# Reading x with features in the partitions, and weaving the first three projections over the tiles of u

## The chip, the cores and the metric

The kernel runs on one core of one Trainium2 chip. The metric is the device time of one execution in microseconds (us). The engines have the names of the profile: PE is TensorE (matmul), PEld its weight loads, DVE is VectorE, ACT is ScalarE, POOL is GpSimd and SP is SyncE, which issues most of the DMAs.

## The reference

One layer of a streaming encoder on 512 frames of 1024 features, float32: a normalised input u, one combined projection of it, three branches (gated linear attention "GLA", forgetting attention "FoX", attention into 256 memory tokens), a gated merge, and a squared-ReLU MLP. What matters here is the head of it.

```python
def rmsnorm(x, g):
    r = lax.rsqrt(jnp.mean(xf * xf, axis=-1, keepdims=True) + EPS)
    return (xf * r) * g

u = rmsnorm(h, g_mix[l])                 # h = x, 512 x 1024
proj = u @ w_in[l]
(gq, gk, gv, gg, ga, fq, fk, fv, ff, mq, gates) = split_cols(proj, PROJ_SIZES)
log_a = jax.nn.log_sigmoid(ga @ w_alpha_up[l] + b_alpha[l]) / GLA_TAU
log_f = jax.nn.log_sigmoid(ff + b_forget[l])      # decay of FoX
...
mkv = rmsnorm(mem, g_mem[l]) @ w_mem_kv[l]        # memory keys and values
mk, mv = jnp.split(mkv, 2, axis=-1)
```

## The kernel before

All matrix products are done in three passes of a short float format: each operand is split into a high part (a cast on ACT) and a low part (operand minus high part, on DVE), and PE adds high x high, high x low and low x high in PSUM. Weights come in chunks of 128 x 1024 numbers (512 KB), in the order of `chunk_list()`: a DMA on SP's queue writes a tile `raw` (three buffers, or two of the tag `lead`), ACT writes `hi` or `whi`, DVE writes `lo` or `wlo` (three buffers each).

The head of the kernel, with which this change deals, has these parts.

- Memory keys, `mem_keys` (L380): chunks 0 to 3, 96 matmuls of 256 columns.
- Memory values, `mem_values` (L394): chunks 4 to 7. For each chunk PE does two units of four matmuls with the high part and two units of two matmuls with the low part, 48 matmuls in all. A unit ends at a `yield`, so other code can decide how many units run between two of its own steps (`run(islice(mv, 2))`).
- u. x is read frame by frame (`xn`: 128 frames in the partitions, four tiles). ACT squares a tile and sums it along the row (L330), DVE and POOL make the factor (mean plus epsilon, to the power of -0.5; L333 and L334), and DVE scales the tile by a factor that is one number for each partition (L340). PE then turns it (L408): 32 transposes of 128 x 128, four for each of the eight tiles `k` of 128 features. ACT and DVE write `uhi` and `ulo` from PSUM (L411, L412), with the gain `g_mix` that is then one number for each partition.
- `g_proj` (L504, L505): the columns of the decays (chunk G: `ga` and `ff`), 16 matmuls. It comes when all of u is there. Then `fox_pair(0)` by `gT` and `mm3` (L157 to L159): the first 128 query columns and the first 128 key columns of FoX (fq, fk), 24 matmuls each. Then `decay_logs` (L520) and FoX's values (fv, four chunks).

PE runs its instructions in the order in which the code is written. On the other engines a scheduler sets the order, which `issue_after` and helpers like `behind` bind in places. `hold[0]` names an instruction on ACT after which later casts of weights are put. `next_sum` lets one sum of weights in DRAM (POOL's queue) go with each cast of a chunk from the 12th call on; they serve the MLP.

Of the kernel before, what the change touches and what calls it, by code (L numbers as in the profile page):

```python
# [32 lines left out]
def chunk_list():  # L33

    L = []
    for c in (0, 512):
        L += [("N", "w_mem_kv", 2 * j, c) for j in range(4)]
    L += [("G",)]
    L += [("T", "w_in", OFF["fq"]), ("T", "w_in", OFF["fk"])]
# [24 lines left out]
def hybrid_block(ctx, tc, chunks, wst, memT, xN, gffn, gfin, wup, cst, out):  # L64
# [57 lines left out]
    def next_sum(after):  # L122
# [3 lines left out]
        if n <= 11:  # L126
            return
        for to, src, add_ in islice(sums[len(late_on)], 1 + (len(late_on) == 1)):
            with tc.issue_after(merged[0]) if late_on else ExitStack():
                if add_:  # L130
                    d = nc.gpsimd.dma_start(to, src, accum_op=ALU.add, max_dma_last_dim=8192)
                else:
                    d = nc.gpsimd.dma_start(to, src)
            tc.add_manual_dep(d.ins, after.name, mybir.DependencyInfo(mybir.DependencyClass.Sync, mybir.DependencyReason.DATA),
                              reason="pace")

# [16 lines left out]
    def get_w(key):  # L153
        return split_w(load_w(key))
# [98 lines left out]
    with pool("front") as fp:  # L253
# [4 lines left out]
        xn = fp.tile([P, NT, D], F32, name="xn")  # L258
        ssx = small(fp, NT, "ssx")
# [61 lines left out]
        load, act, vec = next(lead(chunks[4], after=(load, act, vec)))  # L321

        def x_load(t):
            with behind(load):
                return nc.sync.dma_start(xn[:, t, :], xN[t * P:(t + 1) * P, :]).ins

        def x_square(t):
            sq = fp.tile([P, D], F32, tag="xsq", name=nm("xsq"), bufs=2)
            with behind(act):
                a = nc.scalar.activation(sq, xn[:, t, :], AF.Square, accum_out=ssx[:, t:t + 1]).ins  # L330
            ms, r = (fp.tile([P, 1], F32, tag=g, name=nm(g), bufs=2) for g in ("ms", "rr"))
            with behind(vec):
                m = nc.vector.tensor_scalar(ms, ssx[:, t:t + 1], 1.0 / D, EPS, op0=ALU.mult, op1=ALU.add).ins  # L333
            nc.gpsimd.tensor_tensor(r, ms, mhalf[:, :1], op=ALU.pow)  # L334
            return a, m, r

        def x_scale(t, r, cols=(0, D)):
            for sl in (slice(a, b) for a, b in zip(cols, cols[1:])):
                with behind(vec):
                    v = nc.vector.tensor_scalar(xn[:, t, sl], xn[:, t, sl], r, None, op0=ALU.mult).ins  # L340
            return v

        for t in range(2):
            load = x_load(t)
            act, vec, r = x_square(t)
            if t == 0:
                vec = x_scale(t, r)
        load, act, vec = next(lead(chunks[5], after=(load, act, vec)))
        load = x_load(2)
        act, vec, r2 = x_square(2)  # L350
        vec = x_scale(1, r)
        vec = x_scale(2, r2)
        load = x_load(3)
        act, vec, r = x_square(3)
        x_scale(3, r, (0, 2 * P, D))
        x_act = act
        with behind(load):
            nc.sync.dma_start(ident, cst[:, :P])
        get_plain = get_w

        def get_first(key):
            return pre[key] if key in pre else get_plain(key)

        get_w = get_first
# [18 lines left out]
        def mem_values():  # L383
            pss = [at_() for _ in range(2)]
            for j in range(4):
                with behind(u_mid if j == 3 else None):
                    w = [x.rearrange("p (k c) -> p k c", k=2) for x in get_w(("N", "w_mem_kv", 2 * j, 512))]
                for low in range(2):
                    for t, ps in enumerate(pss):
# [6 lines left out]
                        if j == 3 and low:  # L396
                            with tc.issue_after(u_end):
                                nc.vector.tensor_copy(gqT[t], ps)
                        yield

        def k_copies(after, hs):
            with tc.issue_after(after):
                for h in hs:
                    nc.scalar.copy(mk_raw(h), kps[h])

        def turn(pt, k, ts):
            for t in ts:
                nc.tensor.transpose(pt[:, t * P:(t + 1) * P], xn[:, t, k * P:(k + 1) * P], ident)  # L408

        def u_split(pt, k):  # L410
            a = nc.scalar.mul(uhi[:, k, :], pt, gmix[:, k:k + 1]).ins  # L411
            return a, nc.vector.scalar_tensor_tensor(ulo[:, k, :], pt, gmix[:, k:k + 1], f(uhi[:, k, :]), op0=ALU.mult,  # L412
                                                  op1=ALU.subtract).ins
# [3 lines left out]
        k_copies(x_act, (0, 1))  # L417
        mv = mem_values()
        macc, rm, dg = gv[:, 2, :M], gv[:, 1, :2], gv[:, 3, :M]
        msq = [fp.tile([P, 4, M], F32, name=f"msq{h}") for h in range(2)]  # L420
        u_act = None
        run(islice(mv, 8))
        pts, u_mid = [at_() for _ in range(2)], None
        for ts in (range(NT - 1), (NT - 1,)):
            for k in range(2):
                turn(pts[k], k, ts)
        for k in range(KT):
            if k > 1:
                pts.append(at_())
                turn(pts[k], k, range(NT))  # L430
            u_act, u_end = u_split(pts[k], k)
            u_mid = u_act if k == 3 else u_mid
            u_late = u_act if k <= 5 else u_late
            if k in (1, 3, 5):
                run(islice(mv, 2))
            if k in (5, 7):
                h = k // 7
                with tc.issue_after(u_act):
                    nc.scalar.activation(msq[h], memr[:, 4 * h:4 * h + 4, :], AF.Square)
        k_copies(u_act, (2, 3))  # L440
        run(mv)
        hold[0] = u_late
        get_w = get_plain
# [1344 lines left out]
```

## Time and profile before

| | us |
|---|---|
| median of 3 runs | 815.97 |
| lowest and highest | 814.61, 816.88 |
| the profiled execution, its own time | 815.5 |
| its span | 813.7 |

The span runs from the first to the last instruction of the trace. The profiled execution's own time is 1.8 us longer than its span. All "us" in lines of the profile are counted from the start of the span. In a line of the timeline the first two numbers are the start and the length. Matmul lines overlap, since their ends are modelled; where the time that PE spends is wanted, take the difference of two starts. In the profile's names `T<-a,b` means that T is written from a and b.

### The profile page before, as it was taken

The numbers are of one execution on the slowest core, as the hardware profiler recorded it, in microseconds if no ns is written. First come the engines' busy times: TensorE is split into PE (matmuls) and PEld (weight loads), VectorE is DVE, ScalarE is ACT, GpSimd is POOL, SyncE is SP. The second block draws the span as 40 slices with busy tenths as digits, with TensorE's granted clock in tenths as the row PEclk, the third lists the DMA queues.
The fourth block names the chain that finished last, engine by engine and source line by source line (L and its number), as shares of the span: only waits on it lengthen the run. The fifth ranks groups of instructions, "written<-read, shape, count | busy, mean of one in ns | idle before, by whom it ended". The sixth has DMA issues, their size and how long they took to land.

```text
span 813.7 us, 12505 instructions
## 1 busy us (share of the span) xinstructions
PE 803.3 (99%) x4813; PEld 706.9 (87%) x4813; DVE 591.3 (73%) x913; ACT 442.0 (54%) x699; POOL 109.0 (13%) x135
## 2 busy tenths in 40 slices
PE   8999999999999999999999999999999999999996
PEld 7788888888888888999999889987998899889984
DVE  5856878546455587877567468788788778887896
ACT  7745655543344334444454346874676367637764
POOL 0000110011101112134144110011001100100011
PEclk9999999999999999999999999999999999999998
DMA  9534666688888877767768733998758966896643
GB/s 354 168 118 139 190 177 200 184 236 200 252 236 273 232 227 184 170 165 196 199 148 225 247 98 130 279 233 232 239 163 200 222 210 167 194 281 193 160 82 125
DMA packets 39484, 161.29 MB, mean 198 GB/s; under 512 B 4736, under 2 KB 5184, under 8 KB 37056
## 3 DMA queue, kind: packets, MB, share of 16 engines
q0 software_dynamic: 9776, 58.20, 34.3%
q1 hardware_dynamic: 27856, 97.55, 34.1%
q10 hardware_dynamic: 1792, 4.75, 1.7%
q8 instruction: 37, 0.61, 0.3%
q14 instruction: 23, 0.19, 0.1%
HBM read 158.35 MB, written 35.68 MB: 238 GB/s over the span
## 4 chain that ended last, share of the span: by engine, by line
PE 92%; DVE 3%; ACT 2%; DMA 2%; issue 1%; POOL 0%; POOLq 0%; DVEq 0%; ACTq 0%
PE mm L1233 18%; PE mm L157 17%; PE mm L158 17%; PE mm L159 17%; PE a L157 5%; PE a L158 4%; PE a L159 4%; PE mm L380 1%; PE a L394 1%; DMA b<-in_wst_dram 1%; ACT hi L1357 1%; DVE lo L1291 1%; PE a L624 1%; DVE h L1285 1%; PE a L662 1%
## 5 line engine op out<-in xcount | busy, mean ns | idle before, releaser
L148 DVE TENSOR_TENSOR wlo<-raw,whi 128x1024 fp32r<-128x1024 f32 x65 | 84.1, 1296 | 58.4 <-ACT whi L147 58.2
L157 PE MATMUL mm<-uhi,whi 128*128 128x512 f32 (+1 forms) x352 | 125.8, 357 | 0.0
L159 PE MATMUL mm<-uhi,wlo 128*128 128x512 f32 (+1 forms) x352 | 123.7, 351 | 0.0
L158 PE MATMUL mm<-ulo,whi 128*128 128x512 f32 (+1 forms) x352 | 123.6, 351 | 0.0
L147 ACT CAST whi<-raw 128x1024 fp32r<-128x1024 f32 x65 | 68.4, 1052 | 89.2 <-PE mm L158 54.4
L1289 ACT CAST hi<-raw 128x1024 fp32r<-128x1024 f32 x56 | 58.8, 1050 | 45.1 <-PE mm L1233 30.2
L1291 DVE TENSOR_TENSOR lo<-raw,hi 128x1024 fp32r<-128x1024 f32 x56 | 68.5, 1223 | 14.6 <-ACT hi L1289 14.6
L157 PEld LDWEIGHTS mm<-uhi,whi 128*128 128x128 f32 x352 | 66.7, 189 | 9.9 <-issue 1.5
L159 PEld LDWEIGHTS mm<-uhi,wlo 128*128 128x128 f32 x352 | 66.6, 189 | 9.1
L158 PEld LDWEIGHTS mm<-ulo,whi 128*128 128x128 f32 x352 | 66.7, 189 | 8.1
L1233 PE MATMUL mm<-u2l,hi 128*128 128x256 f32 x240 | 66.1, 283 | 0.0
L1233 PE MATMUL mm<-u2h,hi 128*128 128x256 f32 x240 | 66.1, 283 | 0.0
L1233 PE MATMUL mm<-u2h,lo 128*128 128x256 f32 x240 | 61.1, 283 | 0.0
L1643 POOL DMA_DIRECT2D b<-in_wst_dram x30 | 25.6, 854 | 264.2 <-DVE lo L1291 153.3
L1289 ACT CAST hi<-b 128x1024 fp32r<-128x1024 f32 x36 | 37.8, 1049 | 38.1 <-PE mm L159 24.0
L158 PE MATMUL mm<-lo,ch 128*128 128x512 f32 x136 | 53.0, 390 | 0.7 <-DVE lo L1291 0.7
L157 PE MATMUL mm<-hi,ch 128*128 128x512 f32 x136 | 52.9, 389 | 0.0
L159 PE MATMUL mm<-hi,cl 128*128 128x512 f32 x136 | 52.9, 389 | 0.0
L1233 PE MATMUL mm<-u2sh,hi 128*128 128x256 f32 x192 | 52.6, 283 | 0.0
L1233 PE MATMUL mm<-u2sl,hi 128*128 128x256 f32 x192 | 52.5, 283 | 0.0
L1291 DVE TENSOR_TENSOR lo<-b,hi 128x1024 fp32r<-128x1024 f32 x36 | 43.9, 1221 | 10.4 <-ACT hi L1289 10.2
L1233 PE MATMUL mm<-u2sh,lo 128*128 128x256 f32 x192 | 47.5, 283 | 0.0
(423 smaller groups left out, 2105.7 us busy)
## 6 DMA issues: line engine op xcount, KB each, us to landing
raw<-in_wst_dram SPq DMA_DIRECT2D x113, 512.0 KB
raw<-T SPq DMA_DIRECT2D x32, 512.0 KB
b<-in_wst_dram POOLq DMA_DIRECT2D x32, 512.0 KB, 5.6
T<-in_wst_dram POOLq DMA_DIRECT2D x12, 1024.0 KB, 9.0
b<-in_wst_dram SPq DMA_DIRECT2D x16, 512.0 KB
wb<-in_wst_dram POOLq DMA_DIRECT2D x15, 512.0 KB, 5.4
T<-in_wst_dram POOLq DMA_DIRECT2D x12, 512.0 KB, 5.7
wb<-in_wst_dram SPq DMA_DIRECT2D x8, 512.0 KB
```

The lines of the kernel that those rows point to most:

```text
L147: cast = nc.scalar.copy(hi, raw)
L148: low_now[0] = nc.vector.tensor_tensor(lo, raw, f(hi), op=ALU.subtract).ins
L157: nc.tensor.matmul(ps, lh, rh, start=start, stop=False, skip_group_check=on)
L158: nc.tensor.matmul(ps, lh, rl, start=False, stop=False, skip_group_check=on)
L159: nc.tensor.matmul(ps, ll, rh, start=False, stop=stop, skip_group_check=on)
L380: nc.tensor.matmul(kps[h], w[:, h * P:(h + 1) * P], x[:, k, :], start=k == p == 0, stop=k == KT - 1 and p == 2)
L394: nc.tensor.matmul(ps, x[:, k, sl], w[low][:, kk, :], start=k == low == 0 and x is mxh, stop=k == KT - 1 and low == 1)
L624: nc.tensor.matmul(ps[e], q[a, sl], k[a, :w], start=p == 0, stop=p == 2)
L1233: nc.tensor.matmul(ps[:, a, :], x[:, a, k, :], y[:, s, k, :], start=start, stop=stop, skip_group_check=go is not None)
L1289: nc.scalar.copy(hi, raw)
L1291: nc.vector.tensor_tensor(lo, raw, f(hi), op=ALU.subtract)
L1643: nc.gpsimd.dma_start(to[i], wst[index["B", q, i, x]], accum_op=ALU.add)
```

## The change

x is given twice, as before (`xN`, for the residual) and with features in the partitions (`xT`). The head of the kernel reads `xT` into `xt` (eight tiles of 128 features x 512 frames, two to a DMA), so u needs no transposes. In exchange, the sum of squares runs over partitions:

- ACT squares `xt` (four DMAs' worth; the last in two halves) and DVE adds the eight tiles into one (`x_sum`, L346 and L350 of the new kernel).
- PE adds that tile's partitions, by four matmuls with a column of ones (L429), DVE adds epsilon (L430), and POOL makes all four factors of a partition in one instruction (`rx`, L431). PE then makes of them a row that stands in all partitions (`rb`, four transposes of a broadcast column, L436).
- DVE multiplies each tile of `xt` by `rb` (`x_scale`, L440), ACT writes `uhi` (L443), DVE writes `ulo` (L446).

The projections of fq, fk and G, which were done one after the other, are woven: as soon as tile k of u is there, PE does the matmuls of fq and fk with it (high weights only, L602), and from k = 2 on also the two matmuls of G with tile k-2 (L514, L515). The low weights of fq and fk come last, eight matmuls each (L611). The weights fq, fk and G are loaded and cast earlier. DVE, ACT and SP run in this part in the order in which the code is written (`in_order`, which existed before and is moved up). The copies of the memory values go from DVE to ACT. `hold[0]` is now the copy of the decay columns, and `next_sum` starts at the eighth call, because four chunks no longer go through `split_w`.

```diff
-    L += [("G",)]
     L += [("T", "w_in", OFF["fq"]), ("T", "w_in", OFF["fk"])]
+    L += [("G",)]
...
-        if n <= 11:
+        if n <= 7:
...
-        def x_square(t):
-            sq = fp.tile([P, D], F32, tag="xsq", name=nm("xsq"), bufs=2)
-            with behind(act):
-                a = nc.scalar.activation(sq, xn[:, t, :], AF.Square, accum_out=ssx[:, t:t + 1]).ins
...
+        order = in_order()
+        order.__enter__()
+        next(lead(chunks[4], after=(load, act, vec)))
+        def x_load(j):
+            nc.sync.dma_start(xt[:, 2 * j:2 * j + 2, :].rearrange("p k t -> p (k t)"), xT[j])
+        def x_square(j):
+            sq = fp.tile([P, 2, S], F32, tag="xsq", name=nm("xsq"), bufs=3)
+            for k in range(2) if j == 3 else [slice(0, 2)]:
+                nc.scalar.activation(sq[:, k], xt[:, 2 * j:2 * j + 2, :][:, k], AF.Square)
+            if j == 1:
+                nc.vector.tensor_tensor(sq, sq, sqs[0], op=ALU.add)
...
+        vraws = [fp.tile([P, 1024], F32, tag="lead", name=nm("raw"), bufs=2) for _ in range(2)]
+        nc.sync.dma_start(vraws[0], wst[6])
+        nc.sync.dma_start(ident, cst[:, :P])
+        nc.sync.dma_start(vraws[1], wst[7])
+        fraws = [load_w(("T", "w_in", OFF[n])) for n in ("fq", "fk")]
+        g_raw = load_w(("G",))
...
-        def turn(pt, k, ts):
-            for t in ts:
-                nc.tensor.transpose(pt[:, t * P:(t + 1) * P], xn[:, t, k * P:(k + 1) * P], ident)
...
+        lead_w(chunks[6], vraws[0])()
+        run(islice(mv, 9))
+        lead_w(chunks[7], vraws[1])()
+        ps = at_()
+        for t in range(NT):
+            nc.tensor.matmul(ps[:, t:t + 1], ssum[:, t * P:(t + 1) * P], ones[:, 0:1], start=True, stop=True)
+        nc.vector.tensor_scalar(ms, ps[:, :NT], 1.0 / D, EPS, op0=ALU.mult, op1=ALU.add)
+        nc.gpsimd.tensor_tensor(rx, ms, mhalf[:, :NT], op=ALU.pow)
+        k_copies(range(4))
+        run(islice(mv, 3))
+        rb = at_()
+        for t in range(NT):
+            nc.tensor.transpose(rb[:, t * P:(t + 1) * P], rx[:, t:t + 1].to_broadcast([P, P]), ident)
+        lows = [lead_w(chunks[8 + n], fraws[n]) for n in range(2)]
...
         for k in range(KT):
+            x_scale(k)
+            u_high(k)
+            if k:
+                u_low(k - 1)
+            if k == 1:
+                gw = wp.tile([P, 1024], F32R, tag="hi", name=nm("whi"))
+                nc.scalar.copy(gw, g_raw)
+            if k == 3:
+                nc.vector.tensor_tensor(gw3[:, :, 64:], gr3[:, :, 64:], f(gw3[:, :, 64:]), op=ALU.subtract)
+        u_low(KT - 1)
+        run(islice(mv, 2))
...
+        def first_pair():
+            for k in range(KT):
+                for u in (uhi, ulo):
+                    if k == 0:
+                        run(islice(mv, 1))
+                    for w, ps in zip(ws, pss):
+                        nc.tensor.matmul(ps, w[0][:, k, :], u[:, k, :], start=k == 0 and u is uhi, stop=False)
+                if k > 1:
+                    g_tile(k - 2)
...
+            for w, ps, evac in zip(ws, pss, evacs):
+                for k in range(KT):
+                    nc.tensor.matmul(ps, w[1][:, k, :], uhi[:, k, :], start=False, stop=k == KT - 1)
+                evac(ps)
```

How the instructions stand, at three places. First DVE between the low part of chunk 4 and the first low part of u, before. `ms` and `rr` are the mean square and the factor of one tile of 128 frames; `lo_236` is the low part of chunk 5, `wlo_406` that of chunk 6.

```order
L276 TENSOR_TENSOR lo_215<-raw_213,hi_214 128x1024
L333 TENSOR_SCALAR ms_222<-ssx_138 128x1
L340 TENSOR_SCALAR xn<-xn,rr_223 128x1024
L333 TENSOR_SCALAR ms_230<-ssx_138 128x1
L276 TENSOR_TENSOR lo_236<-raw_234,hi_235 128x1024
L333 TENSOR_SCALAR ms_243<-ssx_138 128x1
L340 TENSOR_SCALAR xn<-xn,rr_231 128x1024
L340 TENSOR_SCALAR xn<-xn,rr_244 128x1024
L333 TENSOR_SCALAR ms_252<-ssx_138 128x1
L340 TENSOR_SCALAR xn<-xn,rr_253 128x256
L340 TENSOR_SCALAR xn<-xn,rr_253 128x768
L148 TENSOR_TENSOR wlo_406<-raw_403,whi_405 128x1024
```

The same engine from the low part of chunk 5 (`lo_228`) on, now: `xsq_222` is the sum of squares, `lo_362` and `lo_396` are the low parts of chunks 6 and 7, `a_399` is the PSUM tile of the column sums, `a_418` is `rb`.

```order
L288 TENSOR_TENSOR lo_228<-raw_226,hi_227 128x1024
L350 TENSOR_TENSOR xsq_248<-xsq_248 128x512
L350 TENSOR_TENSOR xsq_222<-xsq_222,xsq_248 128x512
L350 TENSOR_TENSOR xsq_222<-xsq_222,xsq_251 128x512 x2
L416 TENSOR_TENSOR lo_362<-raw_234,hi_361 128x1024
L416 TENSOR_TENSOR lo_396<-raw_235,hi_395 128x1024
L430 TENSOR_SCALAR ms_359<-a_399 128x4
L440 TENSOR_TENSOR xt<-xt,a_418 128x512 x2
L446 SCALAR_TENSOR_TENSOR ulo<-xt,cols_s,uhi 128x512
L440 TENSOR_TENSOR xt<-xt,a_418 128x512
L446 SCALAR_TENSOR_TENSOR ulo<-xt,cols_s,uhi 128x512
```

The low parts of both chunks 6 and 7 now stand ahead of the one `ms`, and from the scaling on DVE alternates between two instructions for each tile of u.

Second PE, where the values' chunk 5 ends and u begins, before (`a_363` and `a_364` are the two tiles of memory values, `a_389` and `a_390` take the first two tiles of u).

```order
L394 MATMUL a_363<-lo_236,mxh 128x512 x2
L394 MATMUL a_364<-lo_236,mxh 128x512 x2
L408 MATMUL a_389<-cst_s,xn 128x128 x3
L408 MATMUL a_390<-cst_s,xn 128x128 x3
L408 MATMUL a_389<-cst_s,xn 128x128
L408 MATMUL a_390<-cst_s,xn 128x128
L394 MATMUL a_363<-whi_405,mxh 128x512
```

And now, from the column sums to the row of factors, in the middle of chunk 6 (`hi_361`, `lo_362`).

```order
L429 MATMUL a_399<-ones,xsq_222 128x1 x4
L403 MATMUL a_366<-hi_361,mxh 128x512
L403 MATMUL a_366<-hi_361,mxl 128x512
L403 MATMUL a_366<-hi_361,mxh 128x512
L403 MATMUL a_366<-hi_361,mxl 128x512
L403 MATMUL a_365<-lo_362,mxh 128x512 x2
L403 MATMUL a_366<-lo_362,mxh 128x512 x2
L436 MATMUL a_418<-cst_s,rx_360 128x128 x4
```

Eight matmuls of the memory values now stand between the column sums and the row, and the rest of the values (chunk 7, 12 matmuls) after it; the 32 transposes are gone.

Third ACT, around the first tiles of u, before (`whi_405` and `whi_451` are chunks 6 and 7, `a_389` and so on are tiles of u in PSUM).

```order
L147 CAST whi_405<-raw_403 128x1024
L411 ACTIVATE uhi<-a_389,cols_s 128x512
L411 ACTIVATE uhi<-a_390,cols_s 128x512
L411 ACTIVATE uhi<-a_417,cols_s 128x512
L411 ACTIVATE uhi<-a_424,cols_s 128x512
L147 CAST whi_451<-raw_449 128x1024
```

And now (`hi_423` and `hi_426` are fq and fk, `whi_434` is G, `gqT` takes the memory values).

```order
L415 CAST hi_423<-raw_239 128x1024
L415 CAST hi_426<-raw_241 128x1024
L443 ACTIVATE uhi<-xt,cols_s 128x512 x2
L456 CAST whi_434<-raw_243 128x1024
L406 COPY gqT_114<-a_365 128x512
L443 ACTIVATE uhi<-xt,cols_s 128x512
L406 COPY gqT_115<-a_366 128x512
L443 ACTIVATE uhi<-xt,cols_s 128x512 x5
```

The cast of G and the two copies of the values now stand between the second and the fourth tile of `uhi`. On all engines the order behind FoX's first values is the one of before.

More of the change, by code (lines that the diff above doesn't have):

```diff
@@ L337, in x_scale @@
[L337 to L348, printed above, removed]
```

181 lines of the change are left out of this document (80 added, 101 removed).

## Prediction

> **What bounds the kernel now.** I read the page first (busy shares, the chain that ended last), then the busy time by stage, then the timeline of the first 50 us engine by engine.
>
> ```profile
> PE 803.3 (99%) x4813; PEld 706.9 (87%) x4813; DVE 591.3 (73%) x913; ACT 442.0 (54%) x699; POOL 109.0 (13%) x135
> ...
> PE 92%; DVE 3%; ACT 2%; DMA 2%; issue 1%; POOL 0%; POOLq 0%; DVEq 0%; ACTq 0%
> ```
>
> The first line is the busy time of each engine, the second the share of each in the chain that ended last. The stages, each line with the stage's bounds, its length, the busy time and count of PE, PEld, DVE, ACT and POOL, the granted clock of PE, the busy share of the DMA engines and GB/s:
>
> ```profile
> 17.40:33.00 15.60, 15.59 (x83) 12.15 (x82) 10.87 (x16) 11.53 (x19) 1.49 (x2) 1.00 0.62 221
> 33.00:47.50 14.50, 14.50 (x66) 12.00 (x66) 10.77 (x14) 6.72 (x12) 0.35 (x2) 1.00 0.55 183
> 47.50:550.00 502.50, 502.50 (x2968) 438.94 (x2967) 342.46 (x590) 250.81 (x434) 81.07 (x92) 1.00 0.70 197
> 550.00:555.00 5.00, 4.26 (x19) 3.21 (x18) 5.00 (x7) 2.07 (x3) 0.85 (x1) 1.00 0.62 207
> 555.00:805.00 250.00, 249.94 (x1575) 227.03 (x1575) 209.03 (x261) 155.07 (x209) 22.41 (x27) 1.00 0.72 192
> 805.00:813.70 8.70, 1.30 (x6) 0.75 (x4) 2.53 (x5) 2.29 (x6) 1.10 (x2) 0.76 0.31 121
> ```
>
> PE is the bound: between 17.4 and 805 us PE waits for 0.8 us in all, 0.74 of them near 550. So whatever PE work leaves the head moves the end by as much, and each us that PE waits in the new head costs a us. Everything behind FoX's first values stands in the same order on every engine, so I let the rest shift as it is, the short wait at 550 included: DVE and transfers that run there start from work that shifts along.
>
> **What leaves PE.**
>
> ```profile
> 17.41 0.39 PE L394 MATMUL a<-hi,mxh 128*128 128x512 f32 x1
> 17.64 0.39 PE L394 MATMUL a<-hi,mxl 128*128 128x512 f32 x1
> ...
> 23.03 1.04 PE L408 MATMUL a<-cst_s,xn 128*128 128x128 f32 x8
> ...
> 32.98 0.40 PE L504 MATMUL mm<-uhi,whi 128*128 128x512 f32 x1
> ...
> 47.50 1.94 PE L520 MATMUL a<-wup_s,gaT 128*128 128x264 f32 x8
> ```
>
> From the first value matmul (17.41) to the first decay matmul (32.98) are 15.57 us. In them lie 48 value matmuls. The first 24 take 23.03 - 17.41 = 5.62 us, 0.234 each; 48 take 11.24. The rest, 4.33 us, is what the 32 transposes cost with the switches and short waits around them. From 32.98 to 47.50 are 64 matmuls of the decays, fq and fk, 0.227 each; the change keeps all 64.
>
> **What comes onto PE.** Four column sums (float32, each recorded as two matmuls) and four transposes of the factors. The nearest rows:
>
> ```profile
> 66.91 0.50 PE L460 MATMUL a<-ones,gv 128*128 128x1 f32 x4
> 67.27 0.49 PE L157 MATMUL mm<-whi,uhi 128*128 128x512 f32 x1
> 67.60 0.40 PE L158 MATMUL mm<-wlo,uhi 128*128 128x512 f32 x1
> ...
> 86.16 0.60 PE L645 MATMUL a<-cst_s,Pt 128*128 128x128 f32 x4
> 86.60 0.27 PE L647 MATMUL a<-cst_s,Pt 128*128 128x128 f32 x1
> ```
>
> Two such sums take 67.27 - 66.91 = 0.36 us, and the next matmul 0.10 more than 0.23; four take 0.72 + 0.10. Four transposes take 0.44, and I add the same 0.10: 1.36 us together. PE's work falls by 4.33 - 1.36 = 2.97 us. That is the most the change can bring.
>
> **When the row of factors is there.** The new chain is: last tile of x, square, sums, column sums, power, row. It competes with chunks 6 and 7 on ACT and DVE.
>
> ```profile
> 19.17 1.06 ACT L330 ACTIVATE xsq<-xn 128x1024 f32<-128x1024 f32 x1 [1.69 <-DMA xn<-in_xN_dram]
> ...
> 20.49 1.06 ACT L330 ACTIVATE xsq<-xn 128x1024 f32<-128x1024 f32 x1 [0.16 <-DMA xn<-in_xN_dram]
> ...
> 22.06 1.06 ACT L147 CAST whi<-raw 128x1024 fp32r<-128x1024 f32 x1
> ```
>
> DMA in the stage from 20 to 22 us, and single instructions of DVE:
>
> ```profile
> 20.00:22.00 2.00, 2.00 (x10) 1.64 (x9) 1.20 (x3) 1.84 (x6) 0.94 (x1) 1.00 1.01 405
> ...
> 17.52 1.23 DVE L276 TENSOR_TENSOR lo<-raw,hi 128x1024 fp32r<-128x1024 f32 x1 [0.82 <-ACT hi L274]
> ...
> 49.69 0.68 DVE L578 TENSOR_TENSOR Kl<-mm,Kh 128x512 fp32r<-128x512 f32 x1
> 50.29 0.42 DVE L522 TENSOR_SCALAR la<-a 128x256 f32<-128x256 f32 x1
> ```
>
> And the power with four numbers per partition, as the profile's answer for its line has it (shortest, median and longest in ns):
>
> ```profile
> L217 POOL TENSOR_TENSOR rr<-ms,mhalf x4: 1005/1034/1842, 284.6 to 313.2; 128x4 f32<-128x4 f32 x4
> ```
>
> The last x tiles are awaited until 19.17 and 20.49: one 512 KB transfer in 1.3 us, as 405 GB/s gives. The order of the loads up to there is unchanged. Chunk 6 follows (21.8; in the trace its cast starts at 22.06 without waiting), then the identity (64 KB) and chunk 7 at about 23.2, fq 24.5, fk 25.8, G 27.1. These landings are estimates from one transfer per 1.3 us.
>
> ACT squares the last tile by 21.6; the last DVE sums (0.60 from start to start) end at 22.8. PE reaches the column sums after 28 value matmuls, at 17.41 + 6.55 = 23.96: no wait. DVE must do the low part of chunk 7 before the mean: landing 23.2, cast to 24.25, low part 1.22 to 25.5, mean 25.65, hand-over 0.16. For POOL's power on 128x4 there are four instances, three near 1.03 and one of 1.84; I take 1.03. The row can start at 26.85. PE, after 0.82 for the sums and eight value matmuls (1.88), is there at 26.66: it waits about 0.2.
>
> **The weave.** The row is visible at 27.45. PE still has eight value matmuls of chunk 7 with high weights, two with low ones and 0.54 for the row, until 29.75. Scaling (0.60) and `uhi` (about 0.6) need 1.2 to 1.3 us, until 28.8: covered by 0.9 us. Then the rates decide.
>
> ```profile
> 69.95 1.33 ACT L478 ACTIVATE mvh<-gqT,gv 128x512 fp32r<-128x512 f32 x2
> ...
> 72.85 0.74 DVE L479 SCALAR_TENSOR_TENSOR mvl<-gqT,gv,mvh 128x512 fp32r<-128x512 f32 x1
> 73.52 1.28 DVE L211 TENSOR_TENSOR V<-mm,V 128x512 fp32r<-128x512 f32 x2
> ```
>
> For each tile DVE needs 0.60 (scaling) and 73.52 - 72.85 = 0.67 (`ulo`), 1.27 us. PE needs four matmuls for k = 0 and 1 (0.91 us) and six from k = 2 on (1.36). So DVE loses 0.36 on PE in each of the first two tiles and gains 0.09 in each later one. Two things fall into the early tiles: on ACT the cast of G (1.05) and two copies (0.5 each) delay `uhi` of tiles 2 and 3, and on DVE the low columns of G (0.6) stand ahead of tile 4's scaling. Going through the four queues instruction by instruction with these durations, DVE has no slack left at tile 2 and PE waits about 0.15 before the first G matmul and 0.35 before `ulo` of tile 3; after that DVE is ahead again. The low weights of fq and fk (DVE, done near 40 and 41.2) come before PE needs them (41 and 43).
>
> What else is moved: the raw buffers of fq and fk stay occupied until about 40, so the first chunk of FoX's values is loaded later than now.
>
> ```profile
> 25.23 7.92 SPq L140 DMA_DIRECT2D raw<-in_wst_dram  x3
> ...
> 26.00:28.00 2.00, 2.00 (x12) 1.40 (x12) 1.19 (x3) 1.39 (x3) 0.00 (x0) 1.00 0.83 260
> 28.00:30.00 2.00, 1.99 (x13) 1.49 (x13) 1.82 (x3) 2.00 (x3) 0.00 (x0) 1.00 0.01 2
> ```
>
> A load issued at 25.23 on an empty queue has moved its bytes by 28 to 28.5. Issued at 40.2, the chunk is there by 43.4, cast by 45.2 (ACT does FoX's queries first), its low part by 46.5; PE needs it at about 46.8. That costs nothing, with little to spare.
>
> **The sum.** -4.33 + 1.36 + 0.2 + 0.5 = -2.3 us, with 0.1 us or so either way for the waits. From the profiled execution's 815.5 this gives 813.2; the median of before, 815.97, is 0.47 higher, and from there it gives 813.7. I predict 813.4.
>
> **A rule that speaks against the change.** The scaling moves from a form that is quick on DVE to one that is not: before, 1024 numbers per partition in 0.75 us, now 512 in 0.68:
>
> ```profile
> 21.64 0.76 DVE L340 TENSOR_SCALAR xn<-xn,rr 128x1024 f32<-128x1024 f32 x1 [0.44 <-POOL rr L334]
> ```
>
> So u's scaling takes 8 x 0.68 = 5.4 us of DVE where it took 3.0. [...]
>
> **The rivals.**
> - *No waits at all.* If `uhi` and `ulo` keep ahead, the whole 2.97 is gained: 812.5. For it: the waits that I find are a few tenths at two spots. Against: DVE's slack is zero at tile 2.
> - *DVE sets the pace of the weave.* If its instructions start only after the full 0.68 and 0.74 (rows of L578 and L479), a tile costs it 1.42 against PE's 1.36: PE waits some 0.06 for each tile on top and longer at tiles 2 and 3, a gain of 1.6: 813.9. Against: the two distances quoted are shorter than the durations.
> - *The row of factors is late by about one transfer or one slow power* (1.84 instead of 1.03): PE waits 0.8 to 1.5 more, 814.0 to 814.7. One of four instances on POOL was slow.
> - *Slower: the loads share the engines instead of queueing.* Chunks 6 and 7, fq, fk and G are now all asked for between about 13.7 and 19 us. If they land together, at about 27, PE stands at chunk 6 for 4 us from 23.0: gain 2.97 - 4.0 - 0.7, that is 817.2. From a landing of chunk 7 near 25.5 on, the change loses. With an idle PE the granted clock also falls: it is 0.76 in the last stage row, where PE is mostly idle. At that clock the matmuls behind the gap take a third longer; for 3 to 6 us of them that is an estimated 1 to 2 us more, up to 819. [...] Against the rival: x arrived tile by tile, 1.3 us apart, with later loads queued.
>
> **How the numbers follow.** 0.3%, 2.45 us, is about what a measurement of this kernel can tell from no change. Chances: forecast 0.44, half of it on each side of that bound; no waits 0.22 (faster); DVE's pace 0.12 and a late row 0.08 (both within 0.3%); shared loads 0.14, nearly all slower by over 0.3% with the clock, 0.02 within. That is faster 0.44, same 0.44, slower 0.12. The range leaves out the shared loads: from 812.5 less half a us of scatter, 812.0, to 814.7 plus the 0.47 of the median and some scatter, 816.0.
>
> **What would show it.** In the new trace: no L408; the decays, fq and fk end and L528 starts near 45.2 instead of 47.50; L436 starts at 26.7 to 27.2, its wait under 0.5 us and ended by POOL; PE's waits in L602 and L514 between 31 and 35 us sum to about 0.5 and are ended by DVE; chunk 7's cast starts near 23.2; behind L528 PE is as full as now. I am wrong if PE waits at chunk 6 (L403), if L436 starts after 28, if waits for DVE go on beyond tile 4, or if the first chunk of FoX's values (L170) makes PE wait.

## The result, and the profile after

The changed kernel takes 812.93 us (median of 6 runs, 812.10 to 813.87) against 816.38 for the kernel before (6 runs, three of them those of the table ahead of the prediction): 3.4 us less, a ratio of 0.996 with a 95% interval of 0.9947 to 0.9973. Six more runs in a later session gave 813.02 and 0.9962 (0.9947 to 0.9977). The profiled execution took 812.1 us, with a span of 810.3 us where it was 813.7. The forecast was 813.4. One execution of all that were timed took 2835 us, one of ten of the kernel with twelve more matmuls; it is left out of that kernel's median.

The timeline of PE in the changed kernel, at the places that the prediction named (start, length, line):

```profile
17.50 0.39 PE L403 MATMUL a<-hi,mxh 128*128 128x512 f32 x1
...
24.04 0.95 PE L429 MATMUL a<-ones,xsq 128*128 128x1 f32 x8
24.85 0.48 PE L403 MATMUL a<-hi,mxh 128*128 128x512 f32 x1
...
26.79 0.60 PE L436 MATMUL a<-cst_s,rx 128*128 128x128 f32 x4
...
32.44 0.73 PE L602 MATMUL mm<-ulo,hi 128*128 128x512 f32 x2
...
34.30 0.73 PE L602 MATMUL mm<-ulo,hi 128*128 128x512 f32 x2
...
45.32 1.94 PE L528 MATMUL a<-wup_s,gaT 128*128 128x264 f32 x8
```

From the first value matmul to L528, the first decay product (called the head from here on) are 27.82 us; before they were 47.50 - 17.41 = 30.09. So the head is 2.27 us shorter. The other 1.2 us of the two spans' difference lie behind it. Of the changed kernel's waits between 17 and 47 us (what waited for what: us in total, times, longest), the rows of PE and its weight loads:

```profile
PEld mm L602 <- DVE ulo L446: 0.9, 2, 0.5
...
PEld mm L514 <- DVE whi L459: 0.3, 1, 0.3
...
PEld a L436 <- POOL rx L431: 0.2, 1, 0.2
```

The prediction had named the row, the first decay columns and `ulo` of tile 3 (counted from 0), each with the engine that ends it here. A wait at `ulo` of tile 2 (0.37 of the 0.9 us, in front of the matmul at 32.44) comes on top. And the shares of the chain that ended last, with the busy time behind the head by stretches (bounds, length, then busy time and count of PE, PEld, DVE, ACT, POOL, PE's granted clock, DMA share, GB/s):

```profile
PE 96%; DVE 2%; ACT 1%; issue 1%; DMA 0%; POOL 0%; POOLq 0%; ACTq 0%; DVEq 0%
```

```profile
45.32:467.00 421.68, 421.68 (x2438) 365.11 (x2437) 282.65 (x509) 195.84 (x346) 73.75 (x82) 1.00 0.72 203
...
540.00:555.00 15.00, 15.00 (x68) 12.43 (x67) 15.00 (x20) 9.30 (x12) 2.56 (x3) 1.00 0.85 181
```

Before, 2% of that chain were DMA and PE stood for 0.74 us near 550. In this execution PE is full there.

### The profile page after: what moved, and what is told of

The parts are those of the page before. It is cut to its first block, busy times and chain, and to the rows that moved or that the text cites. A ratio compares the mean times of both kernels' runs of the same rounds, so it can differ in the third digit from the quotient of the medians.

```text
span 810.3 us, 12460 instructions
## 1 busy us (share of the span) xinstructions
PE 800.9 (99%) x4793; PEld 705.2 (87%) x4793; DVE 596.8 (74%) x917; ACT 443.9 (55%) x698; POOL 107.6 (13%) x132
## 4 chain that ended last, share of the span: by engine, by line
PE 96%; DVE 2%; ACT 1%; issue 1%; DMA 0%; POOL 0%; POOLq 0%; ACTq 0%; DVEq 0%
PE mm L1264 20%; PE mm L170 17%; PE mm L172 17%; PE mm L171 17%; PE a L170 5%; PE a L171 5%; PE a L172 5%; PE mm L390 1%; PE a L403 1%; PE a L655 1%; PE a L693 1%; PE a L692 1%; DVE h L1316 1%; PE a L931 1%; PE mm L602 1%
## 5 line engine op out<-in xcount | busy, mean ns | idle before, releaser
L170 PE MATMUL mm<-uhi,whi 128*128 128x512 f32 (+1 forms) x336 | 119.7, 356 | 0.0
L161 DVE TENSOR_TENSOR wlo<-raw,whi 128x1024 fp32r<-128x1024 f32 x61 | 79.6, 1309 | 53.0 <-ACT whi L160 53.0
L172 PE MATMUL mm<-uhi,wlo 128*128 128x512 f32 (+1 forms) x336 | 117.5, 350 | 0.0
L171 PE MATMUL mm<-ulo,whi 128*128 128x512 f32 (+1 forms) x336 | 117.3, 349 | 0.0
L160 ACT CAST whi<-raw 128x1024 fp32r<-128x1024 f32 x61 | 64.0, 1052 | 80.2 <-PE mm L171 46.5
L170 PEld LDWEIGHTS mm<-uhi,whi 128*128 128x128 f32 x336 | 63.7, 190 | 9.3 <-issue 1.5
L172 PEld LDWEIGHTS mm<-uhi,wlo 128*128 128x128 f32 x336 | 63.6, 189 | 8.5
L171 PEld LDWEIGHTS mm<-ulo,whi 128*128 128x128 f32 x336 | 63.7, 190 | 7.5
```

The costliest lines, as they stand in the source:

```text
L160: cast = nc.scalar.copy(hi, raw)
L161: low_now[0] = nc.vector.tensor_tensor(lo, raw, f(hi), op=ALU.subtract).ins
L170: nc.tensor.matmul(ps, lh, rh, start=start, stop=False, skip_group_check=on)
L171: nc.tensor.matmul(ps, lh, rl, start=False, stop=False, skip_group_check=on)
L172: nc.tensor.matmul(ps, ll, rh, start=False, stop=stop, skip_group_check=on)
```

## The experiments

Twelve further runs were made in three sessions, nine of them of edited kernels. "Head" is always the time from the first value matmul to the first decay product, read as above; "rest" is the span from there on. The table has every profile; the edits and readings follow.

| kernel | head | decay product starts | rest | median time |
|---|---|---|---|---|
| before | 30.09 | 47.50 | 766.20 | 816.38 |
| before, second profile | 30.07 | 47.38 | 766.82 | 815.92 (one run) |
| transposes twice | 32.77 | 50.09 | 765.91 | 818.43 |
| changed | 27.82 | 45.32 | 764.98 | 812.93 |
| changed, second profile | 27.88 | 45.63 | 765.77 | 813.20 (one run) |
| changed, more rounds | 27.83 | 45.72 | 764.98 | 813.02 |
| 12 more matmuls | 29.94 | 47.05 | 766.05 | 815.95 |
| no weave | 33.81 | 51.53 | 766.07 | 819.77 |
| row 1 us late | 29.14 | 46.28 | 765.92 | 813.89 |
| row 2 us late | 30.83 | 48.16 | 765.94 | 814.91 |
| decay columns late | 28.93 | 46.23 | 765.37 | 813.41 (one run) |
| mean squares first | 28.39 | 45.71 | 766.39 | 813.88 (one run) |
| both | 29.37 | 46.67 | 767.33 | 813.58 |
| two waits worked on | 27.61 | 45.41 | 764.99 | 813.34 |

### The kernel before, a second profile (no edit)

> The kernel before, unchanged, looked at a second time. In its first profile PE waited 0.74 us near 551 for a low part on VectorE, which in the chain of waits goes back to a load of 9.07 us issued at 533.3; the changed kernel's profile has no such wait, and its lead over the kernel before grows there from 2.2 to 3.3 us. Theory A (the wait belongs to the kernel: it comes of where the loads stand when PE gets there): a wait of 0.6 to 0.9 us between 545 and 555 again, chain with 2% of DMA, span within 0.5 of 813.7. Theory B (chance of one execution): no wait over 0.2 us there, and a span near 812.6.

Its waits of PE behind the head, in the timeline between 544 and 556 us:

```profile
545.18 0.50 PE L158 MATMUL a<-lo,ch 128*128 128x512 f32 x1 [0.44 <-DVE lo L1361]
...
551.66 0.50 PE L158 MATMUL mm<-lo,ch 128*128 128x512 f32 x1 [0.74 <-DVE lo L1291]
```

The wait of 0.74 us is there again, with a second one of 0.44 ahead of it, and the rest is 0.6 us longer than in the first profile. It is no single accident; but what is lost there in all isn't fixed either.

### Twelve more matmuls in the changed kernel's head

```
+            for _ in range(12):
+                nc.tensor.matmul(pss[0], ws[0][0][:, 0, :], uhi[:, 0, :], start=True, stop=True)
             for k in range(KT):
```

> The changed kernel with 12 more matmuls of 128x512 ahead of the first column tile of queries; their result is thrown away (the first real matmul starts the sum anew). 12 x 0.227 = 2.72 us more of PE, less the 0.5 us of waits for VectorE that go: the FoX values start near 47.5, as in the kernel before, where the changed kernel had 45.32. Everything behind is the changed kernel's order. Theory A (the wait near 550 depends on when PE gets there): it comes back with 0.6 to 0.9 us, and the time is 812.9 + 2.2 + 1.1 = 816.2. Theory B (chance): no wait near 550, time 815.1. Theory C (the other order of the head's loads, not the shift, took the wait away): none either, 815.1, while the kernel before has it in every look.

The head is 2.1 us longer. The median is 815.95, ratio to before 0.9999 (0.9985 to 1.0013): the whole gain is gone, with nothing added but PE's twelve matmuls. PE's wait between 544 and 556 us:

```profile
550.63 0.50 PE L171 MATMUL mm<-lo,ch 128*128 128x512 f32 x1 [0.52 <-DVE lo L1324]
```

It is a little shorter than the 0.6 to 0.9 us of theory A, where theories B and C had none. That speaks against the order of the head's loads (theory C) as the reason of the gain behind the head.

### No weave

```
-            for k in range(KT):
-                for u in (uhi, ulo):
-                    if k == 0:
-                        run(islice(mv, 1))
-                    for w, ps in zip(ws, pss):
-                        nc.tensor.matmul(ps, w[0][:, k, :], u[:, k, :], ...)
-                if k > 1:
-                    g_tile(k - 2)
             run(mv)
-            for k in range(KT - 2, KT):
+            for w, ps in zip(ws, pss):
+                for k in range(KT):
+                    for u in (uhi, ulo):
+                        nc.tensor.matmul(ps, w[0][:, k, :], u[:, k, :], ...)
+            for k in range(KT):
                 g_tile(k)
```

> The changed kernel with the weave undone: the same x with features in the partitions, the same row of factors and the same instructions, but all 16 matmuls of the queries' column first, then the 16 of the keys, then the 16 of the decay columns, after the last two pieces of the memory values. VectorE finishes the low part of tile 7 at about 37.4 us. The queries' 16 matmuls (3.7 us from 30.0) would be done at 33.8 if nothing waited; with a tile every 1.27 us they end at 37.9, so about 4.0 us of waits ended by VectorE, and 32 x 0.23 = 7.4 us more to 45.3 and the low parts 3.7: the FoX values start near 49. Theory of the prediction (the weave hides VectorE's pace): 812.9 + 3.6 to 4.0 = 816.5 to 816.9, slower than the kernel before or equal to it. Rival (the weave is idle cover, VectorE would have been fast enough): 812.9 within 0.7.

819.77 us, ratio 1.0043 (1.0026 to 1.0061): slower than before. The direction is right, the size is not: the head is 6.0 us longer, not 3.6 to 4.0. The waits between 17 and 60 us, and the busy time in 5 us stretches:

```profile
PEld mm L601 <- DVE ulo L446: 5.4, 7, 1.6
...
PE mm L601 <- DVE ulo L446: 1.4, 2, 1.1
```

```profile
30.00:35.00 5.00, 2.88 (x9) 1.25 (x8) 4.47 (x8) 3.59 (x6) 0.00 (x0) 0.92 0.07 10
35.00:40.00 5.00, 4.86 (x9) 2.33 (x10) 4.87 (x8) 3.39 (x6) 0.27 (x2) 0.50 0.24 97
40.00:45.00 5.00, 5.00 (x22) 4.07 (x21) 4.34 (x6) 0.73 (x1) 0.08 (x1) 0.90 0.59 183
```

Three things had been missed. VectorE's last low part ends at 38.9 us already in the changed kernel, not at the expected 37.4. Here it ends near 39.6, in part since the two copies of the memory values now come to ScalarE together, ahead of `uhi` of tiles 2 and 3; these 2.2 us are about what the head exceeds the expectation by. And PE, in pieces here, had a granted clock of 0.50 for the whole stretch from 35 to 40 us, where 9 matmuls run. What that costs by itself isn't shown, since PE waits for VectorE in most of this stretch.

### The row of factors late, by two powers and by one

```
-        nc.gpsimd.tensor_tensor(rx, ms, mhalf[:, :NT], op=ALU.pow)
+        for _ in range(3):
+            nc.gpsimd.tensor_tensor(rx, ms, mhalf[:, :NT], op=ALU.pow)
```

> The changed kernel with the power that makes the row of factors computed three times on GpSimd, the last result the same: two more instructions, 2 x 1.03 us by the first one's row, between the mean squares and the row. The prediction's price for a late row was one for one: PE waits at the four row transposes 0.2 + 2.06 = 2.3 us, all the waits of the weave stay as they are because VectorE starts later by the same: 812.9 + 2.06 = 815.0. Rival (the weave has slack that takes some of it back): below 814.3. If the waits of the weave go away because the weights' casts on ScalarE get ahead meanwhile, 814.6.

814.91 us, where 815.0 was expected from a price of one for one. The profiled execution tells another story. PE's timeline, and its stretches:

```profile
28.79 0.65 PE L437 MATMUL a<-cst_s,rx 128*128 128x128 f32 x4 [2.01 <-POOL rx L432]
29.20 0.48 PE L403 MATMUL a<-hi,mxh 128*128 128x512 f32 x1
29.52 0.49 PE L403 MATMUL a<-hi,mxl 128*128 128x512 f32 x1
29.80 0.63 PE L403 MATMUL a<-hi,mxh 128*128 128x512 f32 x1
30.23 0.63 PE L403 MATMUL a<-hi,mxl 128*128 128x512 f32 x1
30.66 0.63 PE L403 MATMUL a<-hi,mxh 128*128 128x512 f32 x1
```

```profile
25.00:30.00 5.00, 2.99 (x15) 2.19 (x14) 0.90 (x3) 2.03 (x3) 3.05 (x3) 0.97 0.20 68
30.00:35.00 5.00, 5.00 (x17) 3.94 (x16) 4.02 (x7) 3.69 (x6) 0.00 (x0) 0.69 0.00 0
```

Behind the wait of 2.01 us the matmuls of 512 columns come every 0.43 us instead of 0.23. Counted as stretches at half speed, the granted clocks of 0.97 and 0.69 over two times 5 us are 0.3 + 3.1 = 3.4 us, by estimate about 1.7 us of PE on top of the wait. The head is only 3.0 us longer, since the weave has no waits left here: from the first `uhi` matmul to the low weights of fq and fk (L602 and L611 in the changed kernel) it takes 11.4 us instead of 12.1.

The other nine executions have no profile, but their mean clocks fit. 3.4 us at half speed take 0.002 off the mean clock of 814 us. The four executions at 0.998 have spans of 812.3 to 812.7, the six at 0.996 or 0.997 have 813.1 to 814.1. So it is luck that the median meets the one-for-one price. By this reading the late row costs 1.1 to 1.5 us where the clock holds, less than its 2.06, because the waits of the weave go, and 1.9 to 2.9 us where it falls.

With one power more (`range(2)`):

> The changed kernel with the power computed twice: one more instruction of 1.03 us ahead of the row. With three of them PE waited 2.0 us, its clock fell to half for 3.4 us behind the wait in the profile, and the runs' spans fell apart by granted clock: 812.3 to 812.7 at 0.998, 813.1 to 814.1 at 0.996 or 0.997. Theory A (a wait of about 1.2 us does not reach the clock): the granted clock is 0.998 in all runs, the FoX values start 1.0 later than in the changed kernel, at 46.4, and the time is 812.9 + 1.0 = 813.9. Theory B (it does, in part of the runs): some runs at 0.997 or below and up to 1.7 us longer than the others.

```profile
27.71 0.65 PE L437 MATMUL a<-cst_s,rx 128*128 128x128 f32 x4 [1.10 <-POOL rx L432]
28.12 0.47 PE L403 MATMUL a<-hi,mxh 128*128 128x512 f32 x1
28.43 0.40 PE L403 MATMUL a<-hi,mxl 128*128 128x512 f32 x1
28.67 0.40 PE L403 MATMUL a<-hi,mxh 128*128 128x512 f32 x1
```

813.89 us, 1.0 above the changed kernel: one for one, with matmuls at full pace behind the wait and 1.00 as the granted clock of every stretch from 20 to 40 us. Theory A holds, but for the clock that it expected at 0.998 in all runs. Nine of the ten spans are 811.4 to 812.4, at 0.997 and 0.998 alike; the tenth, 815.0, has a clock of 0.998, so it isn't the clock's. (The head is 1.3 us longer, not 1.0, since here it began at 17.14 instead of 17.50 to 17.89. The row comes with the loads, not with PE, so the earlier PE waits the longer; the decay products start at 46.28, 0.6 to 1.0 later than in the changed kernel.)

### The changed kernel, a second profile (no edit)

> The changed kernel, unchanged, looked at a second time. In five profiles so far (the kernel before twice, three variants of the changed one) PE loses 0.2 to 1.7 us between 540 and 555; only the first profile of the changed kernel lost nothing there. The later GpSimd issued the first load of b near 520, counted from the FoX values' start, the more was lost: 474.58 us in the changed kernel and nothing, 475.6 in the kernel before and 1.1. Theory A (the change moves that issue): nothing lost again, issue within 0.2 of 474.6, span within 0.5 of 810.3. Theory B (that issue falls somewhere else in each execution): 0.5 to 1.2 us lost there, span 811.0 to 811.6, while the FoX values start at 45.3 as before.

Nothing is lost near 550, but here 0.8 us go at another place. The waits between 400 and 800 us, and the stretch:

```profile
PEld mm L171 <- DVE wlo L161: 1.0, 1, 1.0
```

```profile
467.00:470.00 3.00, 2.44 (x11) 1.72 (x10) 3.00 (x6) 1.79 (x5) 0.00 (x0) 1.00 0.83 221
```

Neither theory had that place. The issue near 520 came 475.7 us behind the decay products, and still nothing was lost near 550. Counted as the expectation counts, the link from the issue to the loss fails.

Counted from PE's place behind the loss at 467, it doesn't. From the first transposes of `un` (L1249, at 480.51 here and 479.38 in the first profile) to that issue are 40.81 us here and 40.52 to 40.83 in the three profiles of the table without any loss (two of the changed kernel, and the one with two waits worked on). Of the other ten profiles, the kernel before included, one has 40.70 and loses 0.3 us behind that place; nine have 40.85 to 41.69 and lose 0.4 to 2.3. So, but for the one, a late issue and a loss near 550 go together. Whether one makes the other, or both come of something earlier, is not shown.

### Decay columns later, mean squares earlier, and both

```
-            if k == 1:
+            if k == 4:
                 gw = wp.tile(...)
...
-            if k == 3:
+            if k == 5:
                 nc.vector.tensor_tensor(gw3[:, :, 64:], ...)
...
-                if k > 1:
-                    g_tile(k - 2)
+                if k > 4:
+                    g_tile(k - 5)
             run(mv)
-            for k in range(KT - 2, KT):
+            for k in range(KT - 5, KT):
                 g_tile(k)
```

> The changed kernel with the decay columns three tiles later in the weave: their cast on ScalarE and their low part on VectorE stand behind tiles 4 and 5 instead of 1 and 3, and each tile of them five tiles behind the queries' and keys' instead of two. The prediction's theory: the waits of PE for ulo (0.9 us, 2) and for the decay columns' low part (0.3 us) come of these two instructions; without them they sum to less than 0.2 and the FoX values start at 44.8 to 45.0 instead of 45.32. Rival (VectorE's pace of 1.27 us a tile against PE's 0.91 without the decay columns): PE catches up with VectorE at tile 3 or 4 all the same, the waits stay at 0.6 or more.

The theory fell and its rival holds. The waits between 17 and 47 us:

```profile
PEld mm L602 <- DVE ulo L446: 2.3, 4, 1.1
...
PE mm L602 <- DVE ulo L446: 0.7, 1, 0.7
```

The head is 1.1 us longer. Without the decay columns' two matmuls a tile, PE needs 0.91 us where VectorE needs 1.26. The cast and the low part that I took for the cause of the waits are out of the way, but the decay columns' matmuls went with them, and these were what kept PE behind VectorE.

```
-        lead_w(chunks[7], vraws[1])()
+        low7 = lead_w(chunks[7], vraws[1])
...
         nc.vector.tensor_scalar(ms, ps[:, :NT], 1.0 / D, EPS, op0=ALU.mult, op1=ALU.add)
+        low7()
         nc.gpsimd.tensor_tensor(rx, ms, mhalf[:, :NT], op=ALU.pow)
```

> The changed kernel with the mean squares ahead of the low part of the last memory-value weights on VectorE, not behind it: 25.33 was their start, the column sums end at 24.9. The power and the row come 0.3 us earlier, PE's wait of 0.2 us at the row transposes goes, the waits of the weave stay, the FoX values start 0.2 earlier, at 45.1. Rival: the power's own time on GpSimd (1.0 to 1.8 in different looks) decides, and the start stays within 0.1 of 45.3.

VectorE and GpSimd around the power, in this kernel:

```profile
24.86 0.16 DVE L430 TENSOR_SCALAR ms<-a 128x4 f32<-128x4 f32 x1 [0.77 <-PE a L429]
24.94 1.23 DVE L416 TENSOR_TENSOR lo<-raw,hi 128x1024 fp32r<-128x1024 f32 x1
```

```profile
25.17 1.88 POOL L432 TENSOR_TENSOR rx<-ms,mhalf 128x4 f32<-128x4 f32 x1 [20.33 <-DVE ms L430]
```

and in the changed kernel, where VectorE is idle during the power:

```profile
25.64 1.03 POOL L431 TENSOR_TENSOR rx<-ms,mhalf 128x4 f32<-128x4 f32 x1 [20.59 <-DVE ms L430]
```

The mean squares came 0.5 us earlier, but the power ended 0.4 us later, since it took 1.88 us: it started while VectorE was in a low part, and ended 0.88 us after that (24.94 + 1.23 = 26.17; 25.17 + 1.88 = 27.05). The head is 0.5 us longer than the changed kernel's. Without a VectorE instruction beside it the power took 1.03 in the row above; in the kernel with the row 2 us late three of them took 3.21, 1.07 each, from 25.53 on, with nothing on VectorE between 25.37 and 28. By what means the low part lengthens the power is not shown.

> Both: the decay columns three tiles later and the mean squares ahead of the low part. If the prediction's places for the waits are right, 0.5 + 0.2 us: the FoX values start at 44.6 to 44.8, and the time is 812.9 - 0.6 = 812.3. If VectorE's pace sets it whatever stands between (the rival that the change's end is VectorE's last low part), 812.9.

Both losses add up: the head is 1.5 us longer. The median is nonetheless 813.58, since eight of its twelve spans lie between 811.5 and 812.1; the profiled one (814.0) is among the long ones, with PE waiting 0.8 and 0.7 us for low parts at 545 and 551. A span of 811.6 with this head would leave a rest of 764.9, as short as the shortest of the table; the short ones have no profile that could tell.

### Two waits worked on from the other side

```
-                            nc.scalar.copy(gqT[t], ps)
+                            with tc.issue_after(highs[4 + t]):
+                                nc.scalar.copy(gqT[t], ps)
...
+                    if k == 3 and u is uhi:
+                        g_tile(1)
-                if k > 1:
+                if k > 1 and k != 3:
                     g_tile(k - 2)
```

`highs` holds the instructions that write `uhi`.

> The changed kernel with the waits of the weave worked on from the other side than in the run with late decay columns: there PE, without the decay columns' matmuls to fill, ran into VectorE's pace (3.0 us of waits for ulo). Here the decay columns' tile 1 comes ahead of the low part of tile 3 and not behind it (0.47 us of PE that is ready), and the two copies of the memory values leave ScalarE's queue ahead of uhi of tiles 2 and 3 for places behind tiles 4 and 5 (0.5 us each). Theory: the wait of 0.5 us for ulo of tile 3 goes, those before it shrink to 0.3 together; the FoX values start 19.78 us (now 20.1 to 20.2) after the first piece of the chunk-7 weights' column, that is at 45.0 instead of 45.3 to 45.6; time 812.9 - 0.3 = 812.6, which these rounds can't tell from 812.9. Rival: the waits only move to tiles 4 and 5, the FoX values start as before.

```profile
PEld mm L605 <- DVE ulo L449: 0.6, 2, 0.4
...
PEld mm L517 <- DVE whi L462: 0.3, 1, 0.3
```

The head is 27.61 us, 0.2 shorter than in any profile of the changed kernel, where 0.3 was expected; of 1.2 us of weight-load waits in the weave 0.9 are left. The time, 813.34 (ratio to before 0.996, 0.9946 to 0.9974), can't be told from the changed kernel's. It beats the kernel before, not the changed one.

### The changed kernel in more rounds (no edit)

> The changed kernel unchanged, for the rest of its gain. At the FoX values it leads by 1.8 to 2.2 us in four pairs of profiles; by medians of spans it led by 3.1 (811.2 against 814.3). Theory A (behind the FoX values only chance differs): over these rounds the lead shrinks to 2.2, spans' median 812.1, time 814.0. Theory B (the loads near 520 come better to pass in the changed kernel): the lead stays at 3.0 or more, median 811.3, time 813.0.

Theory B's number came out: 813.02, spans' median 811.25 against 814.2. Over the sessions the spans' medians are 811.2 (13 runs) and 814.2 (61 runs): 3.0 us, of which the head explains 2.2.

### The transposes of before, each issued twice

```
-                nc.tensor.transpose(pt[:, t * P:(t + 1) * P], xn[:, t, k * P:(k + 1) * P], ident)
+                for _ in range(2):
+                    nc.tensor.transpose(pt[:, t * P:(t + 1) * P], xn[:, t, k * P:(k + 1) * P], ident)
```

> The kernel before with each of the 32 transposes of x issued twice: 32 more of the instructions that the change removes. By the prediction's term (4.33 us for 32 of them beside the matmuls between) PE is 4.3 us later at the FoX values, 51.8 instead of 47.4 to 47.5, and the time 816.2 + 4.3 = 820.5. If the transposes were partly cover for waits (for uhi, ulo or x), part of it would have been idle: below 819.5. If the waits near 550 depend on when PE gets there, the rest of the program may differ by up to 1.2 either way.

Only 2.7 us more in the head, and 818.43 in time, 1.9 above before; the rival with part of the cost idle is right. A group of 16 in this kernel's timeline, and its wait between 17 and 49 us:

```profile
22.94 1.91 PE L409 MATMUL a<-cst_s,xn 128*128 128x128 f32 x16
```

```profile
PEld a L409 <- DVE ulo L413: 0.2, 1, 0.2
```

In the kernel before (second profile) the same wait, between 17 and 60 us, was

```profile
PEld a L408 <- DVE ulo L412: 1.3, 4, 0.4
```

Sixteen take 1.91 us, of which the last one's own length is 0.27: 0.109 from one to the next, 3.5 us for 32. So 32 more transposes take 3.5 us of PE, and the head grew by 0.8 less: the waits for VectorE's low parts went from 1.3 us of weight loads to 0.2, filled by the added transposes. The other 0.8 us of the 4.33 were such waits.

## Why the prediction was right

**The sum.** -2.3 us was forecast for the head; two profiles of the kernel before and three of the changed one give -2.2 to -2.3. Its terms landed, but for the make-up of one: column sums at 24.04 without a wait (23.96 forecast), the row at 26.79 (26.7 to 27.2), short gaps at the low parts of tiles 2 and 3 and one at the decay columns (the one at tile 2 was not in the forecast), then none, L528 at 45.32 ("near 45.2"). PE is full from there to 467 us, so the late first chunk of FoX's values cost nothing: from the decay products to its second matmul, with the low weights, are 2.01 us, as before.

**What the 4.33 us were.** The prediction called them what the transposes cost "with the switches and short waits around them". The total was right. The doubled transposes show the parts: 3.5 us of PE, switches included, and about 0.8 of waiting for `ulo` in the old order. The prediction's reading that PE waits for 0.8 us in all, 0.74 of them near 550, misses these: PE's busy time is full there, and only the rows of its weight loads show the waits. The change takes away both parts; the waits of its own order (0.5 + 0.2) stand apart in the sum.

**The pace of VectorE.** The rival with 1.42 us a tile is out. The tiles' rows of the changed kernel:

```profile
33.50 0.75 DVE L446 SCALAR_TENSOR_TENSOR ulo<-xt,cols_s,uhi 128x512 fp32r<-128x512 f32 x1
34.16 0.68 DVE L440 TENSOR_TENSOR xt<-xt,a 128x512 f32<-128x512 f32 x1
34.76 0.74 DVE L446 SCALAR_TENSOR_TENSOR ulo<-xt,cols_s,uhi 128x512 fp32r<-128x512 f32 x1
```

0.66 and 0.60 from start to start, 1.26 a tile, with the scaling's operand `a`, the row, in PSUM. The kernel without the weave and the one with late decay columns show that the weave is needed and the decay columns with it: 6.0 and 1.1 us of head without them.

**The loads.** They queued as assumed; chunk 7's cast starts at 22.99 (forecast near 23.2), so the slower rival did not arise. Its 1 to 2 us for a lowered clock take 3 to 6 us of slow matmuls as given, a length that no row of before shows; behind a gap of 2.01 us, in the kernel with the row 2 us late, it was 3.4 us at half speed by the count above, about 1.7 us.

**Where it missed.** The step "I let the rest shift as it is, the short wait at 550 included" failed: the rest was 0.8 us shorter by the spans' medians, and that is the difference between the -2.3 of the sum and the -3.0 to -3.4 measured; it also decided on which side of the bound of 0.3% the time fell. That the time came within 0.5 us of the forecast is in part luck: from 816.38, the median of six, the sum gives 814.1, and the rest brought it down. The rest is no constant. In fourteen profiles it takes 765.0 to 767.3 us, and what it takes above 765.0 goes mostly near 467 and between 541 and 555 us, where PE waits for low parts on VectorE. In the two places read, the casts ahead had waited for weights: in the first profile of the kernel before, ScalarE stood for 2.24 us until the weights cast at 542.45 were there, in the second profile of the changed kernel for 7.67 us until those at 462.99. Twelve matmuls of padding brought a loss back. The three profiles without any loss are among the five whose decay products start before 45.8; none of the nine later ones is without. That points to PE's place in time against the loads, but it is not shown: the kernel with both edits starts its decay products at 46.67 in its profile, and most of its spans are as short as the changed kernel's. What decides in one execution between 765.0 and 767 stays open. Nor is the order behind FoX's first values quite the one of before: ScalarE does one cast of these values (L160, at 54.23) ahead of four other instructions (L542), where it stood behind them, and VectorE its low part likewise. PE waits for neither.

**Prices that the text gave and no term used.** The late row at one for one holds for a wait of 1.1 us; at 2.0 the lowered clock added an estimated 1.7 in the one profile. A power of 1.84 us, of which the late-row rival had one instance in four, is hardly chance: in the first profile of both kernels the same instance takes 1.84. It had a neighbour on VectorE: it started during a low part (at 313.22 in the kernel before, the low part from 312.98 to 314.20; at 311.07 in the changed kernel, 310.83 to 312.05), and the other three, 1.00 to 1.04, did not. The row's power has no neighbour in the changed order: 1.03 in its first two profiles.

## What to carry to other kernels

Where PE is full, count the work that leaves PE from one fixed instruction to another on its timeline, waits included, and walk the new order through every engine's queue: that gave the head to 0.1 us. Before work is moved away because it stands ahead of an awaited instruction, ask whether it is also what keeps the waiting engine busy. And leave the part of the program that "only shifts" a tolerance of its own, taken from a second profile: here it was as large as a quarter of the gain.

## What the hardware showed beyond that

Behind a single gap of 2.01 us (row 2 us late) PE's granted clock was 0.97 and 0.69 over two stretches of 5 us in the profiled execution, 3.4 us if it was at half speed there, and by the mean clocks some of the nine others had a slow stretch too. Behind a gap of 1.10 us (row 1 us late) it was 1.00 in the profile, and nine of the ten spans show no sign of a slow stretch. With PE in pieces (no weave: 2.88 us busy of 5) the clock was 0.92, 0.50 and 0.90 over three stretches of 5 us, by the same count 6.8 us at half speed, without any wait over 1.6 us.

And GpSimd's power, started during a two-tensor operation of VectorE, took 1.88 us instead of 1.03, in the kernel with the mean squares first and in the one with both edits. Beside a one-tensor operation it was longer too: in the kernel before, the power on one number per partition took 0.94 us where it started during a scaling (L340, 20.44 to 21.19) and 0.55 the other three times. So the order on VectorE was part of what the chain through GpSimd cost in these kernels.
